# Moving the last group's scan into the chunk order of a hybrid gMLP / Mamba-2 kernel

## Chip, cores and metric

The kernel runs on one core of one Trainium2 chip. Its time is the device time of one execution in microseconds (us); times quoted for a kernel are the median of several executions. The profile is a trace of one further execution. TensorE (PE) does the matrix products and writes to PSUM; VectorE (DVE), ScalarE (ACT) and GpSimd (POOL) do the element-wise work; SyncE (SP) issues most of the DMA transfers. Every engine works through its own list of instructions in order and waits at an instruction whose inputs or buffers are not ready.

## The reference

Two layers on a sequence of 1024 tokens with 1024 features, each `h = h + W_out(mixer(RMSNorm(h)) * silu(z))`, and a last RMSNorm, all in float32. Layer A is a causal spatial gating mixer. Layer B, the one that matters here, is a Mamba-2 mixer with 2048 inner features in 8 groups of 256 (4 heads of 64), a state of 128 and chunks of 128 tokens. Cut to what the change touches:

```
z, xbc, dt = split(h @ w_in)                       # z: the gate, 8 groups x 256
xbc = silu(conv4(xbc))                             # x (256), B (128), C (128) for each group
per group and chunk of 128 tokens:
  w   = (C B^T) * exp(decay) * dt                  # causal, 128 x 128 for each of 4 heads
  y   = w x  +  (C state) * exp(cs)  +  x * d_skip
  state = state * chunk_decay + B^T (x * dt * decay_to_end)
g   = y * silu(z)
g   = g * rsqrt(mean(g^2 over the group's 256) + eps) * norm_w
out = g @ w_out                                    # 2048 -> 1024
```

## The kernel before

**Precision and products.** Every large product is done in split float32: an operand is cut into a high and a low part (`split`, lines 107 to 112: ACT casts the high part, DVE or POOL subtracts to get the low one), and `mm3` (lines 133 to 136) adds three matmuls, high x high, high x low and low x high. The output projection (class `Out`, line 616 on) is a seven-product scheme of the Strassen kind: the 2048 x 1024 weight and the gated input are cut in quarters, the products are run in the order 1, 7, 2, 6, 4, 5, 3, and sums of quarters are made between them, largely by DMA transfers that accumulate in SBUF (`add`, `b12_plus`, both issued on POOL). One product has four steps `c` with four parts each: 16 parts of six 128 x 512 matmuls. `fetch(n, c)` loads what a product needs: quarters of the gated input from DRAM (`load_a`, tile `ya`, 512 KB each, with a row of group norms `rb` broadcast to 128 partitions) and of the weight (`load_b`, tile `wb`, 1 MB each). `prep(n, c)` splits the operands of a step, one step ahead of its matmuls.

**The scan.** Groups 0 to 6 go through 56 chunks (`scans`, line 1570), group by group. A chunk has on PE the transposes and `C B^T` (`pe_a`, run two chunks ahead), then `pe_b` with the products with `w`, with the state and the state's own update. Its decay row is a DMA that broadcasts 2 KB to all partitions (`load`, line 1410, tile `wl`, 256 KB, three buffers of the tag `k2`), issued on SP at the end of the chunk three before. ACT makes the exponentials (`decay`, two chunks ahead), DVE multiplies (`weights`, one chunk ahead), forms `tokens` (two ahead), updates the state (`update`) and the output (`out`); POOL adds, carries the state and multiplies with the gate (`gate`).

**Filling.** Between the parts of a chunk, `scans` runs `project`: the input projections of x, B and C of the four groups 2, 4, 6 and 7 (`projections`, line 1274), eight items of 16 units, each unit six 128 x 512 matmuls into the two `acc2` buffers of PSUM. The first 16 units are run ahead; the other 112 are spread evenly over the 56 chunks, two to a chunk. The convolution of each item is a queue of small jobs (`drain`), one ACT scale, three DVE taps (`tap`, line 1205) and a silu, of which one is taken for each chunk.

**The last group.** After the 56 chunks, group 7 has a stage of its own. `z_last` (line 1354) computes its gate: 96 matmuls, into the tile `Z`, which stays in SBUF. `last_steps` (line 1542) is its scan of eight chunks, with all element-wise work on DVE. `bo_first` (line 1707) is products 1 and 7 of the output projection. A small loop at lines 1717 to 1728 mixes the three: three gate steps, loads for two steps of product 1 (`fetch(11, c)`), five steps of gate and scan together, and then the rest of the scan spread over the 32 parts of products 1 and 7 (`interleave`). This part is outside the manual schedule, so the compiler may put its instructions earlier. `into_end` (line 1730), again in written order, runs products 2, 6, 4, 5 and 3, the last norm and the stores. In it, `load_a` multiplies each quarter with its norms on DVE (line 1683) in the very place where it issues the load; for group 7 the source is `Z` itself.

**Buffers.** Most large tiles (operands `hh`/`hl` of the projections, x and B/C of a group, gate tiles `ze`, `ya`, `wb`) share 16 buffers of 8 KB a partition under the tag `s8`; `rb`, the chunk tile `cw` and the squares `gsq` share six of 4 KB under `q4`.

## Time and profile before

| What | us |
|---|---|
| median of 3 runs | 1625.0 (1624.87 to 1628.37) |
| profiled execution, its own time | 1622.94 |
| its span | 1621.2 |
| PE busy | 1514.6 |
| DVE busy | 1085.5 |
| ACT busy | 757.0 |
| POOL busy | 466.8 |
| scan of groups 0 to 6 | 1089 to 1381 |
| gate and scan of group 7 with products 1 and 7 | 1381 to 1490 |
| products 2, 6, 4, 5, 3 and the end | 1490 to 1621 |

The span is the time from the first to the last instruction in the trace. A row of the timeline gives start, duration, engine, source line, operation, output and input, and in brackets how long the engine had been idle before it and what released it. A row of the windows view gives a stretch of the span, and for PE, weight loads, DVE, ACT and POOL the busy time with the number of instructions, then the granted clock of TensorE as a share of full speed, the share of time in which the 16 DMA engines had packets in flight (it can pass 1) and the rate. `PE` rows overlap, since matmuls are pipelined: the distance of their starts is what one costs.

### The profile page before, as it was taken

Reading aid. Unit: us, or ns where it says so; the run is one execution under the profiler, and the core shown is the slowest. Engines: PE = TensorE matmul, PEld = TensorE weight load, DVE = VectorE, ACT = ScalarE, POOL = GpSimd, SP = SyncE. Lnnn points to the kernel's source line nnn. Section 1 sums busy time; section 2 is a strip of 40 time slices with the busy share of each in tenths; the row PEclk is TensorE's granted clock in tenths of the full one; section 3 lists DMA queues with packets and bytes.
Section 4 is the critical chain, followed back from the end, with each engine's and each line's share of the span. In section 5 each row is a group of like instructions: output and inputs, shape, how many; then the busy total and the mean of one; then the engine's idle time right before and its main releaser. Section 6 shows DMA issues by size and latency. Waiting matters only on the chain. (4 is left out here: it accounts for less than half of the span.)

```text
span 1621.2 us, 21245 instructions
## 1 busy us (share of the span) xinstructions
PE 1514.6 (93%) x7832; PEld 1246.8 (77%) x7832; DVE 1085.5 (67%) x1669; ACT 757.0 (47%) x1239; POOL 466.8 (29%) x477
## 2 busy tenths in 40 slices
PE   5899999999999999997899998999999999889988
PEld 4799988888888878775678776777777767657776
DVE  6966566666666545577743788587777777657646
ACT  4522232333223345554543454456666576544454
POOL 3601110000000131234203223316766766221231
PEclk9899999999999999998999999999999999979999
DMA  5153333233334999932253222547666665795993
GB/s 171 44 185 135 106 98 109 101 104 109 109 109 167 297 263 238 191 104 65 83 108 113 83 98 85 175 134 206 172 173 183 171 188 143 228 239 179 223 241 113
DMA packets 164872, 244.89 MB, mean 151 GB/s; under 512 B 16048, under 2 KB 96800, under 8 KB 161568
## 3 DMA queue, kind: packets, MB, share of 16 engines
q1 hardware_dynamic: 134672, 166.43, 34.1%
q0 software_dynamic: 20928, 63.45, 17.2%
q10 hardware_dynamic: 9168, 13.64, 2.3%
q8 instruction: 62, 1.02, 0.3%
q14 instruction: 42, 0.34, 0.1%
HBM read 169.23 MB, written 51.18 MB: 136 GB/s over the span
## 5 line engine op out<-in xcount | busy, mean ns | idle before, releaser
L134 PE MATMUL acc<-hh,wh 128*128 128x512 f32 x868 | 345.3, 398 | 14.5 <-ACT wh L111 4.2
L135 PE MATMUL acc<-hl,wh 128*128 128x512 f32 x868 | 342.8, 395 | 4.4 <-DVE hl L989 4.4
L136 PE MATMUL acc<-hh,wl 128*128 128x512 f32 x868 | 342.5, 395 | 3.8 <-DVE wl L112 3.0
L112 DVE TENSOR_TENSOR wl<-wr,wh 128x1024 fp32r<-128x1024 f32 x94 | 122.9, 1310 | 128.8 <-ACT wh L111 128.8
L134 PEld LDWEIGHTS acc<-hh,wh 128*128 128x128 f32 x868 | 165.8, 191 | 52.0 <-DVE u L1240 5.2
L136 PEld LDWEIGHTS acc<-hh,wl 128*128 128x128 f32 x868 | 165.8, 191 | 41.3 <-DVE wl L112 4.8
L135 PEld LDWEIGHTS acc<-hl,wh 128*128 128x128 f32 x868 | 165.9, 191 | 38.7 <-DVE hl L989 4.8
L111 ACT CAST wh<-wr 128x1024 fp32r<-128x1024 f32 (+1 forms) x113 | 116.2, 1030 | 115.8 <-PE acc L135 78.7
L252 ACT COPY u<-acc 128x512 f32<-128x512 f32 x117 | 68.0, 582 | 187.2 <-PE acc L136 185.9
L136 PE MATMUL acc<-wh,hl 128*128 128x256 f32 x448 | 131.3, 293 | 11.5 <-DVE hl L355 11.5
L134 PE MATMUL acc<-wh,hh 128*128 128x256 f32 x448 | 132.1, 295 | 4.2 <-DVE vt L291 2.5
L135 PE MATMUL acc<-wl,hh 128*128 128x256 f32 x448 | 130.7, 292 | 1.1 <-DVE wl L365 1.1
L1424 ACT ACTIVATE wl<-wl,tk 128x128 f32<-128x128 f32 x256 | 82.1, 391 | 88.2 <-DMA wl<-cs_d 87.7
L134 PE MATMUL ab<-hh,wh 128*128 128x512 f32 x256 | 115.5, 451 | 2.2 <-DVE u L1240 2.2
L136 PE MATMUL ab<-hh,wl 128*128 128x512 f32 x256 | 100.8, 394 | 0.0
L135 PE MATMUL ab<-hl,wh 128*128 128x512 f32 x256 | 100.1, 391 | 0.0
L136 PEld LDWEIGHTS acc<-wh,hl 128*128 128x128 f32 x448 | 89.9, 201 | 12.5 <-DVE hl L355 12.5
L134 PE MATMUL bo<-wh,xh 128*128 128x512 f32 x192 | 80.9, 421 | 14.6 <-ACT wh L111 5.7
L134 PEld LDWEIGHTS acc<-wh,hh 128*128 128x128 f32 x448 | 90.0, 201 | 5.2 <-issue 2.9
L112 DVE TENSOR_TENSOR xl<-ya,xh 128x1024 fp32r<-128x1024 f32 x40 | 49.1, 1228 | 64.3 <-ACT xh L111 64.2
L135 PEld LDWEIGHTS acc<-wl,hh 128*128 128x128 f32 x448 | 90.0, 201 | 1.6 <-DVE wl L365 1.4
L605 POOL DMA_DIRECT2D y_d<-y x8 | 4.4, 548 | 291.8 <-DVE y L602 291.8
(316 smaller groups left out, 3379.6 us busy)
## 6 DMA issues: line engine op xcount, KB each, us to landing
wr<-in_a_w_in_dram SPq DMA_DIRECT2D x48, 512.0 KB, 3.6
wl<-cs_d SPq DMA_DIRECT2D x64, 256.0 KB, 3.6
wr<-in_b_w_in_dram SPq DMA_DIRECT2D x30, 512.0 KB, 4.8
ya<-ya POOLq DMA_DIRECT2D x28, 512.0 KB, 14.7
wb<-in_a_w_out_dram SPq DMA_DIRECT2D x10, 1024.0 KB
wb<-in_b_w_out_dram SPq DMA_DIRECT2D x10, 1024.0 KB, 18.2
wr<-in_b_w_in_dram SPq DMA_DIRECT2D x36, 256.0 KB, 4.4
v<-v_d SPq DMA_DIRECT2D x8, 1024.0 KB, 4.9
```

The lines of the kernel that those rows point to most:

```text
L111: nc.scalar.copy(out=hi, in_=src)
L112: return (eng or nc.vector).tensor_tensor(out=lo, in0=src, in1=hi.bitcast(F32), op=ALU.subtract)
L134: nc.tensor.matmul(out=o, lhsT=l[0], rhs=r[0], start=start, stop=False, **kw)
L135: nc.tensor.matmul(out=o, lhsT=l[0], rhs=r[1], start=False, stop=False, **kw)
L136: nc.tensor.matmul(out=o, lhsT=l[1], rhs=r[0], start=False, stop=stop, **kw)
L252: nc.scalar.copy(out=self.u[n][:, i], in_=a)
L605: store = lambda: nc.gpsimd.dma_start(out=y_d[-1], in_=y)
L1424: nc.scalar.activation(wl[:, j, :], wl[:, j, :], AF.Relu, scale=-1.0, bias=tokc(2, c, self.g)[:, j:j + 1])
```

## The change

The scan's order now has 64 chunks, group 7's among them, with its element-wise work on POOL as for the others. Its gate is an item `z` of 16 units among the projections, placed ahead of group 7's x and B/C; the result goes through DRAM (`z_d`) like the other groups' gates, and so does the gated output (`g_d`). The 144 units are spread to be done by chunk 53 (`LAST`). From chunk 55 on, `fill` runs 26 (`FIRST`) of the 32 parts of products 1 and 7 between the chunks, and the last six after the scan. The loads for all four steps of product 1 are issued four units before the projections end, the second weight quarter in two later places, and each weight load is two transfers of half the size. `load_a` only loads; the multiplication with the norms is done by `ready`, called just before the data are used. The third operand sum (`third`) and `b12_plus` have places of their own. All of this is in written order.

```diff
             if self.scale is None:
                 nc.sync.dma_start(out=raw, in_=src)
             else:
-                self.scale(raw, src, g, i)
+                self.raw[i, kh, c] = self.scale(raw, src, g, i)
+
+        def ready(self, *at):
+
+            if at in self.raw:
+                self.raw.pop(at)()
...
             t = self.B[kh, nb, q] = s8([P, 4, 512], "wb")
-            nc.sync.dma_start(out=t, in_=self.wv(kh, nb, q))
+            for h in range(2):
+                nc.sync.dma_start(out=t[:, 2 * h:2 * h + 2], in_=self.wv(kh, nb, q)[:, 2 * h:2 * h + 2])
...
+            self.ready(i, j, c)
             x, y = A(i, j, c), B(k, l, c)
...
-            if n == 1:
-                self.add(x, self.src[c][:, :, 512:1024] if self.scale is None else A(1, 0, c))
+            if n == 1 and self.scale is None:
+                self.add(x, self.src[c][:, :, 512:1024])
...
+        def third(self, c):
+
+            self.ready(1, 0, c)
+            self.add(self.a(0, 0, c), self.a(1, 0, c))
+
         def sums(self, n, c):
 
             A, B = self.a, self.b
             if n == 2:
+                self.ready(1, 1, c)
                 self.add(A(0, 0, c), A(1, 1, c))
...
-    SPILT, AHEAD, LEFT = (0, 1, 3, 5), 16, 4
+    SPILT, AHEAD, LEFT, LAST, FIRST = (0, 1, 3, 5), 16, 4, 53, 26
...
         seq = [(g, kind) for g in plain for kind in ("x", "bc")]
+        seq.insert(-2, (G - 1, "z"))
...
+        def gate(g, m, th, a):
+            zt = k2([P, 512], "zt")
+            nc.scalar.activation(zt, a[:, th, :], AF.Silu)
+            nc.scalar.dma_start(out=z_d[g][:, m, th * 512:(th + 1) * 512], in_=zt)
+
         def push(g, kind, m, a):
+            if kind == "z":
+                queue.extend([lambda th=th: gate(g, m, th, a)] for th in range(2))
+                return 2
...
-    def z_last(Z):
...
-        if g < G - 1:
-            nc.sync.dma_start(out=ze[:, 0:2], in_=z_d[g][:, :, th * 512:(th + 1) * 512])
+        nc.sync.dma_start(out=ze[:, 0:2], in_=z_d[g][:, :, th * 512:(th + 1) * 512])
...
-            if self.g < G - 1:
-                nc.sync.dma_start(out=gd[self.g][:, :, th * 512:(th + 1) * 512], in_=self.z(4 * th, 4))
+            nc.sync.dma_start(out=gd[self.g][:, :, th * 512:(th + 1) * 512], in_=self.z(4 * th, 4))
...
-    def last_steps():
...
+    def gscale(raw, src, g, th):
+        rb = weights(g, th)
+        nc.sync.dma_start(out=raw, in_=src)
+
+        def scale():
+            for m in range(2):
+                V.scalar_tensor_tensor(raw[:, m, :], raw[:, m, :], bnw(2 * g + m, th), rb, ALU.mult, ALU.mult)
+
+        return scale
...
+    def bo_first():
+        def hook(n, c):
+            if (n, c) == (1, 0):
+                for k in (2, 3):
+                    bo.ready(0, 0, k)
+                for k in (2, 3):
+                    bo.fetch(1, k)
+            elif (n, c) == (1, 1):
+                bo.b12_plus(1, 0)
+            if n == 1 and c > 1:
+                bo.third(c - 2)
+            elif n == 7 and c < 2:
+                bo.third(c + 2)
+            if n == 7 and c:
+                bo.fetch(2, c - 1)
+
+        for n in (1, 7):
+            yield from bo.product(n, hook)
 
     def scans():
 
-        chunks = [(g, c) for g in range(G - 1) for c in range(8)]
+
+        chunks = [(g, c) for g in range(G) for c in range(8)]
         N = len(chunks)
-        scan, rs, ran = {}, {}, [0]
-        total = 32 * len(plain)
+        scan, rs, ran = {}, {}, [0, 0]
+        total = 32 * len(plain) + 16
+        first = bo_first()
+
+        def fill(m):
+
+            upto = min(total, AHEAD + (total - AHEAD) * m / LAST)
+            if ran[0] < total - 4 <= upto:
+                project(total - 4)
+                for c in range(4):
+                    bo.fetch(11, c)
+            project(upto)
+            if ran[0] == total:
+                drain(2)
+            if m == LAST + 1:
+                for c in range(2):
+                    bo.ready(0, 0, c)
+                for c in range(2):
+                    bo.fetch(1, c)
+            elif m == LAST + 1.5:
+                bo.prep(1, 0)
+            while ran[1] < FIRST * (m - LAST - 1.5) / (N - LAST - 1.5):
+                next(first)
+                ran[1] += 1
...
         for n, (g, c) in enumerate(chunks):
-            want = lambda f: AHEAD + (total - AHEAD) * (n + f) // N
             at("pe_b", n)
-            project(want(.5))
+            fill(n + .5)
...
-            if p >= 0:
+            if n >= N - 4:
+                sc = scan[G - 1]
+                if c == 4:
+                    sc.squares(0), sc.sum_a()
+                elif c == 5:
+                    sc.sum_b(), sc.sum_c(0)
+                elif c == 6:
+                    half = group_rstd(G - 1, 0, 512)
+                else:
+                    half[0](), half[1]()
+            elif p >= 0:
...
-            project(want(1))
-        project(total)
-        sc = scan[G - 2]
-        drain(len(queue))
-        sc.squares(1), sc.sum_a(), sc.sum_b(), sc.sum_c(1)
...
+            fill(n + 1)
+        sc = scan[G - 1]
+        sc.squares(1), sc.sum_b(2), sc.sum_c(1)
+        return first
...
-    NZ = 3
-    prev = sts[G - 1]
-    prev["Z"] = s8([P, 2, T], "Z")
-    zl = z_last(prev["Z"])
-    last_ssd = last_steps()
...
-    interleave(last_ssd, 9 + NZ, bo_first(), 32)
...
+        for _ in first:
+            pass
         bo.ran = Out.ORDER
```

More of the change, by code (lines that the diff above doesn't have):

```diff
@@ L1394, in __init__ @@
             self.wl, self.tp, self.cw, self.ps, self.state = {}, {}, {}, {}, {}
-            if g < G - 1:
-                gd.append(dr.tile([P, 2, T], F32, name=f"g_d{g}"))
-            else:
-                gd.append(self.st["Z"])
+            gd.append(dr.tile([P, 2, T], F32, name=f"g_d{g}"))
         def x(self, m, c):
@@ L1540, in group_rstd @@
         return guess, tail
-    def last_steps():
-        sc = Scan(G - 1, V)
-        def a(c):
-            sc.load(c), sc.pe_a(c), sc.decay(c), sc.tokens(c), sc.weights(c)
-        a(0)
-        yield
-        for c in range(8):
-            if c < 7:
-                a(c + 1)
-                yield
-            sc.pe_b(c), sc.carry(c), sc.update(c), sc.out(c)
-            last = sc.gate(c)
-            if c == 1:
-                prefetch(G - 1, 1)
-                rs = group_rstd(G - 2, 0, T)
-            if c in (2, 3):
-                rs[c - 2](last)
-            if c % 4 == 3:
-                sc.squares(c // 4), sc.sum_b(), sc.sum_c(c // 4)
-            if c == 3:
-                half = group_rstd(G - 1, 0, 512)
-            if c in (4, 5):
-                half[c - 4](last)
-            yield
+    rbs = {}
@@ new lines, in weights @@
+    def weights(g, th):
+        if (g, th) not in rbs:
+            n = 2 - g % 2 if g < G - 2 else 1
+            t = q4([P, 2, 512], "rb")
+            nc.sync.dma_start(out=t[:, 0:n], in_=rs_d[g:g + n, th * 512:(th + 1) * 512].partition_broadcast(P))
+            for k in range(n):
+                rbs[g + k, th] = t[:, k]
+        return rbs[g, th]
+    def gscale(raw, src, g, th):
[5 more added lines that the diff above has]
+        return scale
```

83 lines of the change are left out of this document (13 added, 70 removed).

## The prediction

> **What bounds the kernel now.** I read the busy table first, then the windows by stage, then, in the stage that the change removes, the timeline of PE and the chain of waits. The page:
>
> ```profile
> span 1621.2 us, 21245 instructions
> PE 1514.6 (93%) x7832; PEld 1246.8 (77%) x7832; DVE 1085.5 (67%) x1669; ACT 757.0 (47%) x1239; POOL 466.8 (29%) x477
> wl<-cs_d SPq DMA_DIRECT2D x64, 256.0 KB, 3.6
> ```
>
> PE has work in 93% of the span, so only the 106.6 us in which it stands still, and the time in which it runs at less than full clock, can be won by a new order. The windows say where these lie (columns: stretch, length, then busy PE, weight loads, DVE, ACT, POOL, then the granted clock, the DMA share and GB/s):
>
> ```profile
> 1089.00:1381.00 292.00, 283.47 (x1743) 215.52 (x1742) 211.60 (x451) 196.43 (x420) 201.71 (x228) 1.00 0.66 174
> 1381.00:1490.00 109.00, 95.73 (x458) 72.49 (x458) 70.35 (x133) 53.05 (x80) 22.35 (x23) 0.91 0.76 213
> 1110.00:1130.00 20.00, 20.00 (x126) 15.29 (x123) 14.77 (x30) 14.47 (x27) 15.59 (x16) 1.00 0.83 213
> ```
>
> The scan of groups 0 to 6 (first row) is bound by PE: 8.5 us of 292 idle, full clock. The stage of group 7 (second row) loses 109 - 95.73 = 13.3 us idle and, at a mean clock of 0.91, another 109 x 0.09 = 9.8 us. In that stage's timeline of PE the long gaps are these three, and two rows of a stretch without gaps give the price of a matmul:
>
> ```profile
> 1419.10 0.80 PE L134 MATMUL bo<-wh,xh 128*128 128x512 f32 x1 [5.49 <-ACT Z L1366]
> 1436.38 0.79 PE L136 MATMUL bo<-wh,xl 128*128 128x512 f32 x1 [2.89 <-DVE xl L112]
> 1443.03 0.39 PE L135 MATMUL bo<-wl,xh 128*128 128x512 f32 x1
> ...
> 1445.30 0.39 PE L136 MATMUL bo<-wh,xl 128*128 128x512 f32 x1
> 1448.62 0.80 PE L134 MATMUL bo<-wh,xh 128*128 128x512 f32 x1 [2.93 <-ACT xh L111]
> ```
>
> Ten matmuls from 1443.03 to 1445.30 are 0.227 us each, so a unit of six is 1.36 us. After each gap the clock is halved for some time, as the fine windows after the first one show:
>
> ```profile
> 1418.00:1420.00 2.00, 0.90 (x2) 0.81 (x3) 0.00 (x0) 1.99 (x4) 0.00 (x0) 0.50 1.10 262
> 1420.00:1422.00 2.00, 2.00 (x7) 1.07 (x6) 1.22 (x1) 0.15 (x1) 0.00 (x0) 0.50 1.11 262
> 1422.00:1424.00 2.00, 2.00 (x11) 1.67 (x11) 0.00 (x0) 0.00 (x0) 0.00 (x0) 0.50 1.09 257
> 1424.00:1426.00 2.00, 2.00 (x10) 1.66 (x9) 1.31 (x4) 1.41 (x1) 0.00 (x0) 0.88 1.12 267
> ```
>
> One such spell costs 0.9 x 0.5 + 2 x 0.5 + 2 x 0.5 + 2 x 0.12 = 2.7 us. What stands behind the gaps is in the chain that ended last: a decay row of the scan, 256 KB, that usually lands in 3.6 us, takes 10 and 24 us here, since it shares the DMA engines with the loads of the output projection.
>
> ```profile
> 1403.21 10.26 DMA wl<-cs_d
> 1423.10 23.52 DMA wl<-cs_d
> ```
>
> **The change, part by part.** The sum is made against the profiled execution, 1622.94 us (span 1621.2 and 1.74 around it), which lies 2.06 under the median; the gain is then taken from 1625.0.
>
> *Moved at no price.* The 96 matmuls of the gate and eight chunks of scan stay what they are. By the window from 1110 on, four chunks take 20 us without idle time, with 48 projection matmuls:
>
> ```profile
> L134 PE MATMUL ab<-hh,wh 128*128 128x512 f32 x16 | 7.3, 456 | 0.0
> ```
>
> This is one of three equal groups; 48 x 0.227 = 10.9 us leave 9.1, or 2.27 us of scan a chunk. With (144 - 16)/53 = 2.42 units a chunk now takes 2.42 x 1.36 + 2.27 = 5.6 us instead of 5.0; with 26/9.5 = 2.74 parts in the last chunks, 6.0. ACT, busy for 196.43 of 292 us, covers such chunks, and so does POOL (201.71) the additions and gates of group 7 that DVE did; without that cover the gate would be late, for which only the squares wait.
>
> *Removed: 23.1 us*, the 13.3 idle and 9.8 of low clock of the old stage.
>
> *Added: the passage from the projections to product 1, 9.0 us.* Between the end of the units (chunk 53) and the first part of product 1 (behind chunk 54) PE has only scan work, 1.5 chunks, since product 1 needs both `acc2` buffers. DVE meanwhile has a queue, in written order:
>
> ```profile
> L1211 ACT ACTIVATE bc<-ab,par 128x1024 f32<-128x1024 f32 x7 | 8.4, 1198 | 0.0
> L1205 DVE SCALAR_TENSOR_TENSOR bc<-ab,par,bc 128x1023 f32<-128x1023 f32 (+2 forms) x20 | 25.4, 1272 | 1.2 <-ACT bc L1211 1.2
> L1442 DVE TENSOR_TENSOR wl<-wl,cw 128x512 f32<-128x512 f32 x53 | 48.0, 906 | 12.3 <-ACT wl L1426 12.0
> L1432 DVE TENSOR_TENSOR cw<-tp,tk 128x256 f32<-128x256 f32 x53 | 22.2, 419 | 4.7 <-PE tp L1419 4.5
> L1483 DVE TENSOR_TENSOR t<-yy,ze 128x256 f32<-128x256 f32 x48 | 19.9, 415 | 4.2 <-PE yy L1454 4.2
> L1486 DVE SCALAR_TENSOR_TENSOR cw<-x,dsk,yy 128x128 f32<-128x128 f32 x46 | 13.7, 339 | 0.0
> L1477 DVE TENSOR_TENSOR state<-sp,state 128x256 f32<-128x256 f32 x42 | 17.8, 424 | 53.2 <-PE sp L1460 45.6 <-POOL ze L1493 6.4 <-POOL gsq L1503 1.3
> L1434 DVE TENSOR_TENSOR cw<-tp,mask 128x128 f32<-128x128 f32 x54 | 15.0, 278 | 0.0
> L1683 DVE SCALAR_TENSOR_TENSOR ya<-ya,par,rb x28: 739/744/1125, 1396.1 to 1506.3; 128x512 f32<-128x512 f32 x28
> L112 DVE TENSOR_TENSOR wl<-wb,wh x48: 1210/1218/1226, 535.1 to 1584.7; 128x1024 fp32r<-128x1024 f32 x48
> ```
>
> First chain: ACT scale 1.20, three taps 3.82, update 0.42, output 0.42 + 0.68, weights 0.91: 7.4 us until chunk 54 can start, of which PE covers 2.27: 5.2 idle. Second: tokens 0.42 + 0.28, four multiplications with norms 2.98, two low parts 2.44: 6.1 us, again less 2.27: 3.8 idle.
>
> *Added: one spell of half clock, 2.7* (ends 2.7 and 5.4, for one or two); the gap of 2.89 above was long enough for one.
>
> The Trainium skill, "TensorE: Matmul & The Clock Gate", Part 1, says that full clock comes back after about 3.4 us of sustained work. By that a spell would cost 1.7, and the sum below would be 1.0 lower; the rows show some 6 us, and they decide.
>
> *Added: the loads ahead of the decay row of chunk 54, 8.0.* `fetch(11, c)` for four steps stands in chunk 51 ahead of that chunk's own load, on the same SP list:
>
> ```profile
> wb<-in_b_w_out_dram SPq DMA_DIRECT2D x7, 1024.0 KB, 18.2
> ya<-g_d SPq DMA_DIRECT2D x12, 512.0 KB, 5.8
> rb<-rs_d SPq DMA_DIRECT2D x6, 512.0 KB
> 1385.00:1392.00 7.00, 7.00 (x33) 5.79 (x32) 4.89 (x4) 5.15 (x6) 0.00 (x0) 1.00 1.01 345
> ```
>
> Eight `ya`, two `wb` and four `rb` are 8.4 MB, 24 us at the 345 GB/s of the last row, where such loads fill the engines. The row's exponentials (2.2 us) and a square (1.1) stand on ACT ahead of the last item's scale, 5.6 us after the issue, so that the two chains above are late by landing + 3.3 - 5.6. Ends: landing in 3.6, late by 1.3; in 23.52, late by 21.2. I take the row nearest in place, the first decay row behind such loads, 10.26: 8.0.
>
> *Added: four silus of the gate with their table switches*, on ACT, each in a `k2` buffer that a decay row would have had. The cover is ACT's slack and the lead of the decay row of two chunks. I take 1; at worst each holds ACT for a landing of 3.6, of which a quarter reaches PE: 4.
>
> *Added: contention in the last chunks, 2.* The second weight quarter, its sum, four third sums, four sums for product 7 and the loads for product 2 are some 17 MB in 65 us, 260 GB/s, and this is what full engines moved in the old stage:
>
> ```profile
> 1420.00:1444.00 24.00, 20.65 (x84) 15.39 (x84) 10.92 (x19) 8.33 (x12) 6.22 (x5) 0.76 1.08 265
> ```
>
> So they just fit. But the `ya` are there before product 1, which takes away the cause of the gaps of 2.89 and 2.93. Ends 0 and 10 (the idle time of this row, 3.4, taken three times).
>
> *Won: longer chunks, 3.* Of the 8.5 us idle in the scan, most are short waits that 0.6 us more PE work a chunk covers. Ends 0 and 5.
>
> *Won: the late multiplication in product 2, 4.7.* Today DVE stands at group 7's second half, and behind it are the low parts of product 6:
>
> ```profile
> 1513.80 1.41 DVE L1683 SCALAR_TENSOR_TENSOR ya<-Z,par,rb 128x512 f32<-128x512 f32 x2 [3.65 <-DMA rb<-rs_d]
> 1515.00:1525.00 10.00, 6.38 (x19) 4.51 (x18) 6.61 (x12) 6.55 (x12) 7.95 (x9) 0.75 1.08 269
> 1525.00:1535.00 10.00, 10.00 (x41) 8.11 (x41) 5.78 (x8) 2.20 (x3) 0.11 (x1) 0.91 1.06 216
> 1520.00:1562.00 42.00, 41.27 (x168) 33.38 (x168) 21.44 (x25) 19.45 (x24) 12.76 (x15) 0.92 1.07 249
> ```
>
> That costs 3.6 idle and 10 x 0.25 + 10 x 0.09 = 3.4 of clock. With `ready` one step later and six parts of product 7 behind the scan it goes. But the stage behind is full of transfers (1.07 in the last row), which start no sooner than their engines are free: I let a third be given back there. Ends 7 and 0.
>
> *Added: 1 for the second trip of group 7 through DRAM.* Its 1 MB of loads costs 4.2 us at 249 GB/s in the full stage; most lies ahead of it. Ends 0 and 4.
>
> Sum: -23.1 + 9.0 + 2.7 + 8.0 + 1 + 2 - 3 - 4.7 + 1 = **-7.1**, so 1625.0 - 7.1 = **1618**.
>
> **Rivals.** *The loads bury the decay row (slower).* The mechanism is the 8.0 above at its far end: the decay row lands behind all 8.4 MB. For it speak 23.52 us in a like place, and 18.2 as the median of the weight loads; against it, that the loads wait for buffers which the projections free one by one, so that they start apart. Late by 21.2 instead of 8.0, with a second cold spell: -7.1 + 13.2 + 2.7 = +8.8, 1634. It decides the sign from a landing of 17.4 us on (late by 15.1). The Trainium skill, "DMA: Bandwidth & Descriptors", Queues, rings and completion order, says that what SP issues shares one ring on each engine and is consumed in ring order, which is this case, and by it the row lands after the 24 us; the 10.26 us, with far less than 8.4 MB ahead, does not speak against it.
>
> *The stalls go almost all.* The decay row lands in time (1.3), no contention, silus hidden, the late multiplication wins 7 and the scan 5: -23.1 + 9.0 + 2.7 + 1.3 - 5 - 7 = -22.1, 1603. For it: the scan itself ran at a DMA share of 0.66 with hardly a gap.
>
> *No change.* The products behind 1490 are limited by their accumulating transfers; nothing of the 4.7 stays and the extra load costs its 4: -7.1 + 4.7 + 3 = +0.6, 1625. For it, the share of 1.07; against it, 41.27 of 42 us with PE busy.
>
> *It doesn't do what it says.* If SP waits at the sixth operand tile for a buffer that only the last units free, loads aren't spread, and it ends like the first rival.
>
> **Numbers.** Forecast 0.39 (its own range 1610 to 1622), stalls gone 0.17, no change 0.14, decay row buried 0.26, the last 0.04. A measurement of this kernel tells 0.2%, 3.25 us, from no change. Faster: 0.36 of the forecast and 0.17, 0.53; same 0.03 and 0.14, 0.17; slower 0.30. The range goes from 1601, just under the second rival, to 1637, just over the first; it leaves out the joint far ends (1655).
>
> **What would show it.** In the changed profile: chunks of 5.6 us without gaps up to chunk 53; a gap of PE of some 13 us at chunk 54, released by the weights on DVE, behind it the chain tap, scale, exponential, decay row, and a second of some 4 us ahead of product 1; no wait for `rb` at product 6. A landing of the decay row over 17 us proves the forecast wrong on one side, a passage of under 9 us idle on the other; gaps in products 6 and 4 longer than before would show the gain given back.

## The result and the profile after

The changed kernel takes 1688.3 us (median of four executions, 1685.8 to 1692.3) beside 1626.7 for the kernel before on the same chip: a ratio of 1.038, 95% interval 1.0354 to 1.0407. It is slower by some 61 us; the forecast was 1618, with a range from 1601 to 1637.

The page of the changed kernel, with the lines that answer to those of before:

```profile
span 1684.1 us, 21308 instructions
PE 1527.7 (91%) x7828; PEld 1253.0 (74%) x7828; DVE 1069.0 (63%) x1646; ACT 765.8 (45%) x1247; POOL 484.6 (29%) x500
wl<-cs_d SPq DMA_DIRECT2D x64, 256.0 KB, 3.8
```

PE stands still for 1684.1 - 1527.7 = 156.4 us instead of 106.6, and is busy for 13.1 more; since the number of matmuls is the same but for four records, this is most likely time at half clock. The decay rows land in 3.8 us in the median, 3.6 before. The windows of the changed kernel, cut at the last matmul of the projections, the first part of product 1 and the end of product 7:

```profile
1089.00:1417.00 328.00, 305.15 (x1787) 232.50 (x1785) 194.40 (x428) 202.55 (x413) 195.74 (x219) 0.98 0.56 151
1417.00:1436.00 19.00, 9.50 (x47) 6.51 (x47) 11.80 (x20) 11.48 (x17) 4.83 (x6) 0.75 0.98 303
1436.00:1536.00 100.00, 74.61 (x358) 55.82 (x357) 56.06 (x107) 43.25 (x77) 41.07 (x48) 0.83 0.72 195
1536.00:1684.00 148.00, 120.20 (x482) 95.22 (x481) 83.89 (x128) 63.51 (x91) 33.32 (x36) 0.90 0.81 199
```

Every stretch is worse than its counterpart. What each loses is its length less the work in it, with the prediction's prices, 1.36 us a unit or part and 2.27 us a chunk; it holds the idle time and the time at low clock together. The scan of before has 290.7 - 8.5 = 282.2 us of work; with three chunks less and 16 units more it is 282.2 - 6.8 + 21.8 = 297.2. From the last projection of x, B and C to the end of product 7 before has the gate's 21.8, eight chunks and 32 parts, 83.5 us, and the changed kernel 11 chunks and 32 parts, 68.5. The ends are the first `yy`, the last `ab` and the first `bo` of product 2 in the timeline of PE.

| Stretch | before: length, lost | after: length, lost | more |
|---|---|---|---|
| scan with projections | 290.7, 8.5 | 327.2, 30.0 | 21.5 |
| to the end of product 7 | 108.7, 25.2 | 119.5, 51.0 | 25.8 |
| products 2, 6, 4, 5, 3 and the end | 131.5 | 147.8 | 16.3 |

The longest waits of PE in the timeline of the changed kernel, one of each kind:

```profile
1187.01 0.50 PE L134 MATMUL ab<-hh,wh 128*128 128x512 f32 x1 [1.90 <-DVE x L1218]
...
1325.29 0.52 PE L1419 MATMUL tp<-ident,xbc 128*128 128x128 f32 x3 [2.76 <-DMA xbc<-xbc_d]
...
1338.21 1.12 PE L1451 MATMUL yy<-wl,cw 128*64 128x128 f32 x8 [4.15 <-ACT srow L1514]
...
1424.68 1.12 PE L1451 MATMUL yy<-wl,cw 128*64 128x128 f32 x8 [5.30 <-issue]
...
1433.37 0.79 PE L134 MATMUL bo<-wh,xh 128*128 128x512 f32 x1 [3.54 <-ACT wh L111]
...
1500.30 1.12 PE L1451 MATMUL yy<-wl,cw 128*64 128x128 f32 x8 [13.80 <-issue]
...
1622.70 0.80 PE L134 MATMUL bo<-wh,xh 128*128 128x512 f32 x1 [7.13 <-ACT wh L111]
```

The two at 1424 and 1433 are the passage to product 1, where the prediction expected two waits. The others stand in places where it expected none in its sum: the first kind comes three times in the scan and twice more at 0.5 to 0.7 us, the next two lie where group 7's gate is projected, 13.80 us is in the chunks that share PE with product 1, and 7.13 us, at the start of product 5, is a gap of the kind that it named as the sign of a gain given back; the kernel before waits 1.34 us there.

### The profile page after: what moved, and what is told of

Read it like the earlier page. It is cut to its first block, busy times and chain, and to the rows that moved or that the text cites. A ratio compares the mean times of both kernels' runs of the same rounds, so it can differ in the third digit from the quotient of the medians.

```text
span 1684.1 us, 21308 instructions
## 1 busy us (share of the span) xinstructions
PE 1527.7 (91%) x7828; PEld 1253.0 (74%) x7828; DVE 1069.0 (63%) x1646; ACT 765.8 (45%) x1247; POOL 484.6 (29%) x500
## 5 line engine op out<-in xcount | busy, mean ns | idle before, releaser
L134 PE MATMUL ab<-hh,wh 128*128 128x512 f32 x288 | 128.6, 447 | 9.3 <-DVE x L1218 4.7
L136 PE MATMUL ab<-hh,wl 128*128 128x512 f32 x288 | 114.2, 396 | 0.0
L135 PE MATMUL ab<-hl,wh 128*128 128x512 f32 x288 | 113.2, 393 | 0.0
L136 PEld LDWEIGHTS acc<-wh,hl 128*128 128x128 f32 x448 | 88.7, 198 | 13.4 <-DVE hl L355 13.4
L111 ACT CAST xh<-ya 128x1024 fp32r<-128x1024 f32 x40 | 42.0, 1051 | 118.2 <-DMA ya<-ya 54.0
L1490 POOL TENSOR_TENSOR cw<-cw,t 128x256 f32<-128x256 f32 x56 | 60.3, 1076 | 105.2 <-DVE cw L1487 90.0
```

Source lines behind the costliest of these rows:

```text
L111: nc.scalar.copy(out=hi, in_=src)
L134: nc.tensor.matmul(out=o, lhsT=l[0], rhs=r[0], start=start, stop=False, **kw)
L135: nc.tensor.matmul(out=o, lhsT=l[0], rhs=r[1], start=False, stop=False, **kw)
L136: nc.tensor.matmul(out=o, lhsT=l[1], rhs=r[0], start=False, stop=stop, **kw)
L1490: self.eng.tensor_tensor(out=t2, in0=t2, in1=t1, op=ALU.add)
```

## The experiments

Times are medians; the ratio is to the kernel before in the same comparison, with its 95% interval. The first four runs each change one thing in the changed kernel.

### Third sums in step with product 1

```diff
-            if n == 1 and c > 1:
-                bo.third(c - 2)
-            elif n == 7 and c < 2:
-                bo.third(c + 2)
+            if n == 1:
+                bo.third(c)
```

> The changed kernel with the four third sums (A00 += A10 by accumulating transfer) issued at steps 0 to 3 of product 1 instead of at steps 2 and 3 of product 1 and 0 and 1 of product 7. Theory (the sums are issued too late for product 7, 14 us of landing against a lead of one step): the gap of 13.8 us of PE ahead of chunk 62 and the ACT wait of 13.0 us before the last step of product 7 go, with the cold spells behind them; 1688 becomes 1665 to 1674. Rival (the DMA engines are full there, the sums land no earlier): 1683 to 1692.

Measured: 1667.6 us, 1.0258 [1.0211, 1.0305], 20.7 below the changed kernel. The reason stands in POOL's timeline. In the changed kernel the third sums of the quarters 0 and 1 are issued in steps 2 and 3 of product 1, the second of them behind a weight sum that waits for ACT:

```profile
1477.70 1.31 POOL L674 DMA_DIRECT2D wb<-in_b_w_out_dram  x1 [4.11 <-ACT wb L673]
...
1479.04 1.76 POOL L709 DMA_DIRECT2D ya<-ya  x1
```

and ACT, which casts the sum for product 7, waits for its landing 15 us later, and again for the last of the four sums:

```profile
1493.65 1.04 ACT L111 CAST xh<-ya 128x1024 fp32r<-128x1024 f32 x1 [11.04 <-DMA ya<-ya]
...
1523.98 1.04 ACT L111 CAST xh<-ya 128x1024 fp32r<-128x1024 f32 x1 [13.04 <-DMA ya<-ya]
```

DVE's low part and the scan's weights stand behind the first of these casts, and PE with its 13.80 behind them. With one sum a step POOL issues them ahead of need, and the wait of 13.80 is gone. Three of POOL's four sums in the run:

```profile
1445.56 0.94 POOL L709 DMA_DIRECT2D ya<-ya  x1 [6.02 <-issue]
1455.64 1.30 POOL L709 DMA_DIRECT2D ya<-ya  x1
1467.83 0.87 POOL L709 DMA_DIRECT2D ya<-ya  x1 [8.30 <-DVE ya L1561]
```

### The late multiplication called early

```diff
                 bo.fetch(2, 2)
+                bo.ready(0, 1, 2)
...
                 bo.fetch(22, 0)
+                bo.ready(1, 1, 0)
```

(and the same for the other steps of `into_end`)

> The changed kernel with the multiplication with the norms put back next to its load within product 2 (the late call of ready undone there). Theory (the late call moves POOL's accumulating transfers behind VectorE's work for product 6, so that their burst starts 13 to 16 us later against the end of product 2): the stage behind product 7 shrinks from 148 to about 135 us, 1688 becomes 1672 to 1679. Rival (the stage is longer because of group 7's extra trip through DRAM and full engines, not because of the order): 1684 to 1692. My forecast had the opposite sign for this part: it would make the kernel 5 us slower.

Measured: 1679.7 us, 1.0328 [1.0287, 1.037], 8.6 below the changed kernel and just above the 1672 to 1679 that the theory gave. The mark is the burst of accumulating transfers that opens product 6, in POOL's timeline of the kernel before, of the changed kernel and of this run:

```profile
1515.74 0.87 POOL L702 DMA_DIRECT2D ya<-ya  x1 [6.41 <-issue]
```

```profile
1579.86 0.87 POOL L709 DMA_DIRECT2D ya<-ya  x1 [13.43 <-ACT wh L111]
```

```profile
1567.85 0.87 POOL L709 DMA_DIRECT2D ya<-ya  x1 [8.07 <-DVE ya L1561]
```

From the burst to the end of the span the three take 105.5, 104.2 and 105.9 us. So what the tail loses, it loses ahead of the burst, which comes 26.0, 43.6 and 34.3 us after the end of product 7: POOL can't issue the sum before DVE has multiplied, and with the multiplication at the place of use DVE has low parts of another product and additions to the output ahead of it, which wait for transfers of their own. The early call brings about half of the delay back, and the wait ahead of product 5 falls from 7.13 to 2.50 us.

### More convolution jobs a chunk

```diff
-            drain()
+            drain(1 if n % 3 else 2)
```

> The changed kernel with four jobs of the convolution taken in three chunks instead of three. Theory (units run at 2.42 a chunk, their convolution jobs at 1 a chunk, so the rest is done in a burst at the next item half and PE waits for the last tap with both PSUM buffers taken: five gaps of 0.7 to 1.9 us, with cold spells): the scan up to the last projection shrinks by 7 to 12 us, 1688 becomes 1676 to 1681. Rival (the scan is slower because of the gate's item, its silus and its buffers): 1685 to 1691.

Measured: 1693.7 us, 1.0416 [1.0378, 1.0454], 5 above the changed kernel. The waits of 1.90 are gone but for one of 0.80 and one of 0.72; in their place stand others, among them 7.26 us for `xbc` at 1336. The theory that a steadier queue of convolution jobs wins the 7.1 us back falls.

### The early loads really early

The test for the early loads, `ran[0] < total - 4 <= upto`, never holds: one half chunk asks for up to 139.2 units, which runs the 140th, and in the next one 140 < 140 is false. So the loads of product 1 go out at chunk 54, not before:

```profile
1419.80 0.43 SPq L1550 DMA_DIRECT2D rb<-rs_d  x1
1420.28 0.55 SPq L1557 DMA_DIRECT2D ya<-g_d  x1
1421.73 3.77 SPq L668 DMA_DIRECT2D wb<-in_b_w_out_dram  x4
```

```diff
-            if ran[0] < total - 4 <= upto:
+            if ran[0] <= total - 4 <= upto:
...
-                for c in range(4):
+                for c in range(2):
                     bo.fetch(11, c)
```

> The changed kernel with the test for the early loads made to hold (it compares the count of units with a bound that the count has already reached, so that the loads never go out there), for two steps of product 1 instead of four, as there are no buffers for four. Theory now: VectorE's waits of 4.8 and 2.1 us for the first gated quarters go, 1688 becomes 1681 to 1686. Theory of my forecast (the decay row of the next chunks lands behind these loads): the gap at chunk 54 grows from 5.3 to 8 or more, 1690 to 1698.

Measured: 1687.4 us, 1.0372 [1.0327, 1.0416]: no difference from the changed kernel that can be told. The trace shows that both effects are there, and that they cancel. In the changed kernel DVE stands for the landing of the first quarter, which is what the wait of 3.54 in the passage goes back to:

```profile
1429.88 1.42 DVE L1561 SCALAR_TENSOR_TENSOR ya<-ya,par,rb 128x512 f32<-128x512 f32 x2 [4.76 <-DMA ya<-g_d]
```

With the loads early this wait of DVE is gone. But now a decay row, issued behind these loads, lands after 9.64 us, and ACT waits for it. The row from the chain that ended last, ACT, and the two waits of PE in the passage:

```profile
1409.93 9.64 DMA wl<-cs_d
```

```profile
1419.60 1.28 ACT L1425 ACTIVATE wl<-wl,tk 128x128 f32<-128x128 f32 x4 [5.68 <-DMA wl<-cs_d]
```

```profile
1429.57 1.12 PE L1451 MATMUL yy<-wl,cw 128*64 128x128 f32 x8 [8.08 <-issue]
...
1436.82 0.66 PE L135 MATMUL bo<-wl,xh 128*128 128x512 f32 x1 [1.79 <-DVE wl L112]
```

The first wait grows from 5.30 to 8.08 us, and the second, 3.54 and 0.66 before, shrinks to 1.79.

### The gate's tiles out of the decay rows' buffers

The next three take up the scan. In the changed kernel SP's timeline at chunk 36, where the x, B and C of group 5 are to be fetched, shows the decay row (`wl`) held for 9.2 us, from 1305.98 to 1315.13, and the fetch behind it:

```profile
1305.04 0.94 SPq L120 DMA_DIRECT2D wr<-in_b_w_in_dram  x2
1315.13 0.34 SPq L1414 DMA_DIRECT2D wl<-cs_d  x1
...
1316.85 1.07 SPq L1386 DMA_DIRECT2D xbc<-xbc_d  x1
```

```diff
-            zt = k2([P, 512], "zt")
+            zt = q4([P, 2, 512], "zt")[:, 0]
```

> Edit: the four tiles of group 7's gate (zt) take a q4 buffer and no longer one of the three k2 buffers of the decay rows. Theory (a zt in the ring of three makes the next decay row wait for the buffer of a chunk that is not done, and SP stands at it with the prefetch of x, B, C behind it): the waits of PE for xbc (2.76, 2.38), srow (4.15) and wl (1.35) in the stretch from 1290 to 1380 of the changed kernel go, with their half clock 8 to 13 us: 1675 to 1681. Rival (the pace of 2.42 units a chunk makes chunks late on DVE, ACT and POOL anyway): within 3 us of the changed kernel, 1685 to 1691.

Measured: 1677.5 us, 1.0313 [1.0289, 1.0337], 10.8 below the changed kernel. The same place of this run:

```profile
1301.42 0.94 SPq L120 DMA_DIRECT2D wr<-in_b_w_in_dram  x2
1304.49 0.34 SPq L1414 DMA_DIRECT2D wl<-cs_d  x1
...
1306.37 1.03 SPq L1386 DMA_DIRECT2D xbc<-xbc_d  x1
```

The row is held for 2.1 us, the fetch goes out 10.5 us sooner (6.9 sooner counted from the operand loads ahead of it), and the waits for `xbc` of 2.76 and 2.38 are gone. A ring of three buffers with one more tenant gives the next decay row the buffer of the chunk that is still running, and SP stands there with all that follows. In the run with more convolution jobs, the 7.26 us for `xbc` stood behind the same thing: SP held a decay row for 14.4 us.

```diff
-            drain()
+            drain(2 if len(queue) > 3 else 1)
```

(with the gate's tiles in q4)

> Edit: the gate tiles in q4 as in the run before it, and after a chunk two jobs of the convolution are taken instead of one while more than three are left. Theory (a half item takes 3.3 chunks now and its queue has four or five jobs, so that the rest is forced out just when the next matmul waits for the accumulator: the waits of 1.90 on DVE x and bc, 7.1 us in all; that the earlier run with more jobs a chunk lost time came from SP standing 14.4 us at a decay row behind zt): 5 to 8 below the run with q4 alone. Rival (more jobs in a chunk put DVE behind its chunk's own work): equal to or above the run with q4 alone.

Measured: 1689.5 us, 1.0379 [1.0355, 1.0402], 12 above the run with q4 alone. That the first such run lost time only through SP is thereby refuted as well: more jobs a chunk put PE behind ACT, as two waits of this run show.

```profile
1169.77 0.66 PE L1451 MATMUL yy<-wl,cw 128*64 128x128 f32 x8 [2.11 <-ACT wl L1427]
...
1276.24 0.66 PE L1451 MATMUL yy<-wl,cw 128*64 128x128 f32 x8 [2.10 <-ACT wl L1427]
```

```diff
-        seq.insert(-2, (G - 1, "z"))
+        seq.insert(2, (G - 1, "z"))
```

> Edit: the gate item stands third among the projections (chunks 7 to 13) instead of seventh (chunks 33 to 40), its tiles still in k2. If the tiles in the decay rows' ring are the cause, the gaps move with them to the earlier chunks and the time stays within 5 us of the changed kernel, 1683 to 1693. If the loss around chunk 36 comes from the place (group 6's x, B and C projected earlier than before, so that the operand buffers are full when group 5 is fetched), the gaps go: 1674 to 1680.

Measured: 1677.2 us, 1.0308 [1.0275, 1.0341]. The gate in another place wins as much as its tiles in other buffers do. This lies in the range that was worked out for the place as the cause, not for the tiles. It fits with a tile in the ring costing nothing by itself, but only where a fetch of x, B and C stands behind the held row; whether the fuller operand buffers of the old place have a part in it, these two runs don't tell apart.

### The three together, and what is left

> Edit: the changed kernel with three edits together: third sums issued one by one within product 1, the late multiplications of group 7 called as soon as their data are fetched (products 2 to 4), and the gate tiles in q4. Theory (three separate causes, each with its own place): the gains add up, 1688.3 - 20.7 - 8.6 - 10.8 = 1648, within 4. Rival (they share one limit, the transfers behind product 1, so that time won ahead is lost there): 1654 to 1665. Above 1632 in both: the rest, some 20 us over the kernel before, would be the passage to product 1 and the remaining scan.

Measured: 1651.1 us, 1.0154 [1.0133, 1.0174]. The gains add up to 37.2 of 40.1, as for three separate causes. Some 25 us over the kernel before are left, and what follows changes this run, but for two runs that change the kernel before. By the reckoning of the table its scan loses 316.4 - 297.2 = 19.2 us, 10.7 more than before, the chunks up to the end of product 7 104.5 - 68.5 = 36.0, 10.8 more, and the tail takes 137.0, 5.5 more; the scan begins 2.3 us later.

```diff
-        seq.insert(-2, (G - 1, "z"))
+        seq.append((G - 1, "z"))
...
-            if c == 4 and g < G - 1:
+            if c == (6 if g == G - 2 else 4) and g < G - 1:
                 prefetch(g + 1, 0)
```

> Edit: the run before it, and the gate item last among the projections instead of ahead of group 7's x, B and C, with group 7's first gate and row loads at chunk 54 instead of 52. Then no convolution stands between the projections and product 1. Theory (the passage's first wait, 5.3 us and its half clock, is the chain of the last B/C item's taps ahead of the weights on DVE): that wait goes, 5 to 9 us below the run with the three edits. Rival (group 7's gate or rows now come late, so that POOL and SP stand at chunks 55 to 57, or DVE's queue was not the cause): equal or above.

Measured: 1670.1 us, 1.0271 [1.0242, 1.0299], 19 above. The wait of 5.31 us in the passage is gone, which bears out its cause, but the first part of product 1 now waits 8.35 us, and in the scan, which ends 14 us later, PE once waits 9.96 us for `srow`. Why the scan suffers from the earlier x, B and C stays open.

```diff
             at("pe_b", n)
+            if n > 0:
+                at("weights", n + 1)
             fill(n + .5)
...
-            if n > 0:
-                at("weights", n + 1)
```

> Edit: the run with the three edits, and in every chunk the weights of the next chunk are written on DVE's list ahead of the filling work and no longer behind it. Theory (what is left over the kernel before is mostly DVE's list in the last chunks: the scan's weights stand behind the norms and low parts of product 1, and these wait for ACT; PE's waits of 5.31, 6.30, 3.16, 1.40 and 1.34 ahead of yy, with their half clock 15 to 25 us): 1651 falls to 1630 to 1640. Rival (the last chunks are limited by the transfers, the decay rows above all, and DVE only by what is left): 1645 to 1652.

Measured: 1656.7 us, 1.0193 [1.0153, 1.0233]: not lower, rather 5.6 higher. With the update of the state moved as well, from chunk 52 on:

> Edit: the run with the three edits, and only from chunk 52 on the weights of the next chunk and the update of the state are both written ahead of the filling work. Theory (DVE's list in the last chunks): as the run before it or 2 to 6 lower, 1626 to 1640, since the state's product waits for DVE as well; if the run before it gains in the earlier chunks too, this one lies above it by that. Rival (transfers): 1645 to 1652.

Measured: 1651.0 us, 1.015 [1.0115, 1.0185], no difference. The same move of the weights in the kernel before:

> Edit: the kernel before, with the weights of the next chunk ahead of the filling work in the 56 chunks of its scan. Its filling work there is only matmuls and convolution jobs, with 8.5 us idle in 292 and full clock, so theory: within 3 us of the kernel before, 1622 to 1630; the order on DVE matters only where the filling work itself puts work on DVE ahead of the chain. Rival (it is the order that costs in any chunk): 1616 to 1621.

Measured: 1632.6 us, 1.0045 [1.0024, 1.0066], 7.5 slower, where I expected nothing. So the written order on DVE was not what the last chunks wait for, and weights ahead of the filling cost time in either kernel.

The early loads once more, now that the third sums are in time:

> Edit: the run with the three edits, and the early loads for product 1 really issued early (the test holds; two steps of four, as many as there are buffers for). Theory (PE's second wait in the passage, 4.21 us on the cast of the weight, is the late landing of the first input quarter, 2.1 to 2.9 us on DVE): 2 to 6 below 1651. Rival (the loads delay the decay rows as much as they help): 1649 to 1655.

Measured: 1650.1 us, 1.0156 [1.0122, 1.019]: nothing again, and by the same two effects. The decay row lands 10.34 us after its issue, the first wait of the passage grows from 5.31 to 8.79 us, and the second shrinks from 4.21 and 0.65 to 1.79.

### Two limits side by side

```diff
-            for m in range(2):
+            for m in range(2 if g > 3 else 0):
                 V.scalar_tensor_tensor(raw[:, m, :], raw[:, m, :], bnw(2 * g + m, th), rb, ALU.mult, ALU.mult)
```

> Edit: the run with the three edits, and the multiplications with the group norms for the eight quarters of groups 0 to 3, which product 1 and the third sums use, left out (16 of 0.71 us on DVE, 11.3 us; the output lacks these norms). Theory (in the chunks with product 1 DVE's list is full: multiplications, low parts and the scan's own work, each low part behind a cast on ACT that waits for the multiplication): 8 to 14 below 1651, 1637 to 1643. Rival (transfers set the pace there): 1646 to 1652.

Measured: 1653.2 us, 1.0176 [1.0151, 1.0201]: no gain from 11 us less on DVE. The trace shows why. Where the run with the three edits has PE waiting for the weights behind DVE's list,

```profile
1449.94 1.12 PE L1451 MATMUL yy<-wl,cw 128*64 128x128 f32 x8 [6.30 <-issue]
```

this one has it waiting longer at the next such place, because ACT waits for a decay row that SP issues at 1437.32, behind loads of `ya` and `wb`. PE first, then ACT, then SP:

```profile
1459.01 1.12 PE L1451 MATMUL yy<-wl,cw 128*64 128x128 f32 x8 [9.83 <-DVE wl L1443]
```

```profile
1450.75 1.28 ACT L1425 ACTIVATE wl<-wl,tk 128x128 f32<-128x128 f32 x4 [10.63 <-DMA wl<-cs_d]
```

```profile
1432.95 3.67 SPq L1557 DMA_DIRECT2D ya<-g_d  x3
1437.32 0.50 SPq L1414 DMA_DIRECT2D wl<-cs_d  x1
```

The row lands 13.4 us after its issue.

So two further runs leave out the rows, alone and with the multiplications:

```diff
-            nc.sync.dma_start(out=t.rearrange("p h l -> p (h l)"), in_=src.partition_broadcast(P))
+            if self.g < G - 1:
+                nc.sync.dma_start(out=t.rearrange("p h l -> p (h l)"), in_=src.partition_broadcast(P))
```

> Edit: the run with the three edits, and the eight decay rows of group 7 not loaded (ACT reads another tile in their place, so that group 7's scan is wrong). Theory (two limits side by side in the chunks with product 1, the rows' landing and DVE's list): little, 1645 to 1651. If the rows' landing alone set the pace there: 1636 to 1643.

> Edit: no rows of group 7 as in the run before it, and no multiplications for groups 0 to 3 as in the earlier run. Theory (two limits side by side): 8 to 14 below 1651, 1637 to 1643, where each alone gave nearly nothing. Rival (a third thing, POOL's list with its sums or the transfers of product 1's own operands): 1646 to 1653.

| | rows loaded | rows of group 7 left out |
|---|---|---|
| multiplications | 1651.1 | 1650.4 |
| multiplications of groups 0 to 3 left out | 1653.2 | 1638.9 |

Each alone gives nothing, both together 12.2 us (ratios 1.0156 [1.0105, 1.0207] and 1.0082 [1.0052, 1.0111]). In the chunks with product 1 the landing of the decay rows and DVE's list are limits of about the same size. The kernel before has these rows and multiplications too, so the 12.2 us say what the two limits hold back, not how much of it came with the change. Without the rows the wait of PE stays as it was:

```profile
1449.27 1.12 PE L1452 MATMUL yy<-wl,cw 128*64 128x128 f32 x8 [6.28 <-DVE wl L1444]
```

### The beat of the scan

```diff
                 drain(len(queue) - last)
+                if kind == "z":
+                    last = push(g, kind, m, H2["A11"][0].bitcast(F32))
+                    prep(i + 1, m)
+                    continue
...
-        total = 32 * len(plain) + 16
+        total = 32 * len(plain)
```

> Edit: the run with the three edits, and the 96 matmuls of group 7's gate left out (silu of another tile takes their place, so that group 7's gate is wrong); the other 112 units are spread over the same 53 chunks, 2.11 a chunk instead of 2.42. The matmuls themselves are 96 x 0.227 = 21.8 us. Theory (the scan's remaining loss of some 13 us is the price of the denser filling: more forced convolution jobs, chains of DVE and ACT that no longer fit): falls by 30 to 36, 1615 to 1621. Rival (the loss is in the chunks' own chains or in the place): falls by 18 to 25, 1626 to 1633.

Measured: 1634.2 us, 1.0059 [1.0038, 1.0081]: 16.8 lower, less than the 21.8 us of the matmuls left out and less than either theory gave. The gate's units cost no more than their matmuls; without them the scan still runs badly. One thing of the change that remains is that the projections end at chunk 53. The last run does that in the kernel before, and nothing else but to leave out a rounding:

```diff
-            want = lambda f: AHEAD + (total - AHEAD) * (n + f) // N
+            want = lambda f: min(total, AHEAD + (total - AHEAD) * (n + f) / 53)
```

> Edit: the kernel before, with its 112 units spread over 53 chunks instead of 56 (2.11 a chunk), so that a half item of eight units takes 3.8 chunks instead of four. Free of waits the stretch from 1089 to the last unit would take some 277 us then. Theory (the scan's remaining loss is the beat between half items and chunks: convolution jobs forced out ahead of a matmul, 1.9 us each, and chunks out of step): 285 us or more, with waits of PE for DVE x or bc, and a time of 1631 to 1642. Rival (the loss comes from something else of the change): 277 to 281, and 1622 to 1630.

Measured: 1637.6 us, 1.0081 [1.0057, 1.0105], 12.6 slower. Its window from the first chunk to the last unit, and two of PE's waits:

```profile
1087.00:1387.00 300.00, 280.32 (x1687) 213.75 (x1687) 194.35 (x430) 189.24 (x400) 192.75 (x216) 0.99 0.59 161
```

```profile
1108.59 0.50 PE L134 MATMUL ab<-hh,wh 128*128 128x512 f32 x1 [1.90 <-DVE x L1205]
...
1257.42 1.12 PE L1450 MATMUL yy<-wl,cw 128*64 128x128 f32 x8 [5.00 <-issue]
```

From the first `yy` to the last unit 53 chunks take 299.7 us where 56 took 290.7; with three chunks less of work, 275.4, that is 24.3 us lost instead of 8.5. At two units a chunk a half item of eight fills four chunks, in which its four convolution jobs go out one by one; at 2.11 it fills 3.8 and at 2.42 only 3.3, so that the last job is forced out just ahead of the matmul that waits for the accumulator, and chunks and items no longer keep step. That the pace matters is shown; that it does so through the jobs is not, since both runs with more jobs a chunk lost time, and which of the small waits comes from which shift stays open.

## Why the prediction was wrong, step by step

The step that failed at the root is the first term: the prediction took all 23.1 us of stalls to go with the old stage, and allowed 2 us for the sums and loads in the last chunks, 1 for the gate's tiles, and a gain of 3 for the denser pace of the scan. The runs give 20.7 us for the place of the third sums on POOL's list, 10.8 for the gate's tiles and 12.6 for the pace.

**The sum of 61 us.** The third sums, 20.7, the multiplications in the tail, 8.6, and the gate's tiles, 10.8, give 37.2 together. Of the rest, 24.4 by the medians and 29.3 by the two profiled spans, the table's reckoning puts 10.7 in the scan, 10.8 in the chunks with product 1, 5.5 in the tail and 2.3 ahead of the scan. For the scan the pace alone, in the kernel before, costs 12.6; for the chunks with product 1 two limits worth 12.2 are shown, but not that the change brought them; the tail and the start no run took up.

**"Removed: 23.1 us."** The old stage is gone, but the stretch that took its place loses 51.0 us by the table, twice the 25.2 of before. Even with the third sums in time and the gate's tiles elsewhere it is 36.0: so the step failed in taking the old stage's waits to go with its loop. That they came from product 1 and a scan side by side, which both kernels have, fits this but is not shown by a run.

**"The passage, 9.0 us."** The size is right: 19 - 9.50 = 9.5 us idle in the window from 1417 on, with waits of 5.30 and 3.54 + 0.66 where 5.2 and 3.8 were worked out. The first has the cause that was given, and the run with the gate last took it away as this predicts. The second met its number by luck: it was to come from four multiplications and two low parts on DVE, but DVE stood 4.76 us for a quarter whose load went out late, and with that load early only 1.79 us are left.

**"One spell of half clock, 2.7."** Their number was wrong, and the size too high. The windows around the first wait of 1.90 in the changed kernel:

```profile
1185.00:1187.00 2.00, 0.10 (x1) 0.00 (x0) 1.81 (x3) 1.13 (x3) 1.30 (x2) 1.00 0.96 278
1187.00:1189.00 2.00, 1.99 (x6) 1.62 (x7) 0.00 (x0) 1.98 (x3) 0.89 (x1) 0.66 0.87 289
1189.00:1191.00 2.00, 2.00 (x7) 1.52 (x6) 0.00 (x0) 1.99 (x2) 1.49 (x1) 0.50 1.05 172
1191.00:1193.00 2.00, 2.00 (x18) 1.43 (x16) 0.00 (x0) 2.00 (x5) 0.00 (x0) 0.99 1.09 179
```

cost 2 x 0.34 + 2 x 0.50 = 1.7 us, not 2.7: a wait of 1.90 nearly doubles itself, and the scan had eight waits of 1.3 us or more. The Trainium skill, "TensorE: Matmul & The Clock Gate", Part 1, has the clock halved after an idle window of about 3.4 us; here 1.90 was enough, and the measurement decides. The same part's 3.4 us of sustained work until full clock comes back, by which the prediction worked out 1.7 for a spell, is nearly met here: PE resumes at 1187.01 and has full clock again at about 1191.0, 4.0 us later.

**"The loads ahead of the decay row, 8.0."** This step failed at its first sentence: the loads don't stand in chunk 51, since the test for them never holds, and in the passage ACT takes the decay row of its chunk at 1418.75 without waiting. The last rival, that the loads do not do what the change says, was true in this, for another reason, yet not what cost the time: with the loads early the time is the same, 1687.4 and 1650.1. The mechanism itself is real, as the runs with two of the four steps early show: the row lands after 9.64 and 10.34 us, close to the 10.26 taken, and the chain of scale, taps and weights behind it is late as described. The price was too high: the two waits of the passage come to 9.9 and 10.6 us then, instead of the 9.0 and 8.0 that were added up. Beside loads that go out late the early ones cost 2.8 and 3.5 us at the first wait and win 2.4 and 3.1 at the second. Two chunks later the decay rows' landing is one of the two limits of product 1's chunks. Alone it decides nothing, so the slower rival, at 1634 nearest to the result, was near for a wrong reason.

**"Four silus of the gate, 1."** The price failed, not the place. I named the buffer that a decay row would have had, and priced only ACT's delay; what it costs is SP held for 9.2 us with the next fetch behind it, 10.8 in all, with the share of the gate's place left open above. The end of 4 was too low as well.

**"Contention in the last chunks, 2."** I costed bytes against a rate, and asked neither where each sum stands on POOL's list nor when the product that needs it begins. ACT stood 11 and 13 us for such sums; 20.7 us in all, outside the ends 0 and 10.

**"Longer chunks win 3"**, and "moved at no price" with it. The sign failed. A chunk took (1416.8 - 1089.6)/53 = 6.2 us instead of the 5.6 forecast. More PE work a chunk brought new waits instead of covering the old ones, in the kernel before as well; the three waits of 1.90 for a forced convolution job alone cost, with the clock behind each, more than the 3 I had hoped to win.

**"The late multiplication wins 4.7."** The sign failed here too. I followed DVE, which is relieved, and not POOL, which issues what waits for the product: the burst of sums starts 43.6 us after the end of product 7 instead of 26.0. The early call gives 8.6 back.

**"1 for the second trip through DRAM"** was not measured by itself.

## What to carry to other kernels

When work is moved, follow not only the engine that does it but every list that waits for its result: an in-order engine that issues transfers (POOL, SP here) passes a late input on to all that stands behind it. Before giving a tile a buffer from a ring, ask which tenant's next buffer that turns into one still in use; and before changing a spread, look for queues that are counted in the old step. Where taking one suspect away wins nothing, take away two: a second limit of the same size hides the first. And where an edit wins nothing, look in its trace before calling it without effect: here early loads won and lost some 3 us each.

## What the hardware showed unexpectedly

In the run with weights and state update ahead, DVE's multiplication of the weights, 0.68 or 0.69 us in most other places, took 4.03 us, and POOL in the same stretch ran five element-wise instructions back to back. DVE first, then POOL:

```profile
1463.53 4.03 DVE L1443 TENSOR_TENSOR wl<-wl,cw 128x512 f32<-128x512 f32 x1
```

```profile
1463.00 0.99 POOL L1490 TENSOR_TENSOR cw<-cw,t 128x256 f32<-128x256 f32 x1
1463.69 0.86 POOL L1469 TENSOR_TENSOR state<-state,tk 128x256 f32<-128x256 f32 x1
1464.27 0.85 POOL L1438 TENSOR_TENSOR cw<-cw,tk 128x256 f32<-128x256 f32 x1
1464.84 0.96 POOL L1494 TENSOR_TENSOR ze<-ze,cw 128x256 f32<-128x256 f32 x1
1465.52 1.49 POOL L1503 TENSOR_TENSOR gsq<-gsq 128x512 f32<-128x512 f32 x1
```

DVE ends at 1467.56, half a microsecond after the last of them at 1467.01. The Trainium skill, "SBUF — State Buffer", SBUF: two separate sides, says that a pair of ports shared by the two is an exclusive lock: of a DVE operation with two SBUF inputs and a GpSimd operation that reads SBUF, whichever starts first has it for its whole instruction, and the other waits. These rows would fit with DVE waiting for several POOL instructions in a row; no run tested it by itself.
